# Token-major projections in chunks of 512 columns instead of 256, one PSUM bank for each block of 128 tokens

## The chip, the core and the metric

The kernel runs on one core of one Trainium2 chip. The metric is the device time of one execution in microseconds (us). In what follows PE is TensorE, DVE is VectorE, ACT is ScalarE, POOL is GpSimd and SP is SyncE, whose queue issues the DMAs.

## The reference, cut to what matters

Four layers work on 512 tokens of 1024 features in float32: an even mixer, a retention mixer and two hybrid mixers, each followed by a gated convolutional feed-forward network. Every layer begins with a normalisation of the features and ends with a residual. What matters here are the projections at the head of each mixer and the attention that reads them:

```python
# even mixer
proj = xn @ w_in
q, k, v, gate_b, gate_c, h = jnp.split(proj, ...)
q = rms_norm(heads(q), q_gain); k = rms_norm(heads(k), k_gain)
a = dilated_attention(q, k, heads(v))
b = gate_b * causal_dwconv(gate_c * h, sconv_w)
return jnp.concatenate([a, b], axis=-1) @ w_out
# retention mixer
o = chunkwise_retention(rotary(xn @ wq), rotary(xn @ wk), xn @ wv)
return (jax.nn.silu(xn @ wg) * group_norm(o)) @ wo
# hybrid mixer (two layers)
q_nsa, kv_nsa, g_nsa, qkv_sb, g_merge = jnp.split(h @ w_in, cuts, axis=-1)
o_nsa = nsa_attention(rope(q_nsa), ...)        # compressed + selected + window, gated
o_sb = stick_breaking_attention(*qkv_sb)
g_a, g_b = jnp.split(jax.nn.sigmoid(g_merge), 2, axis=-1)
y = g_a * (o_nsa @ w_proj_nsa) + g_b * (o_sb @ w_proj_sb)
return y @ w_out
```

## The kernel before, in words

The kernel is written in stages: mix0, ffn0, mix1, ffn1, hyb0, glu0, hyb1, glu1. The activations stand transposed in SBUF, as eight tiles of 128 features by 512 tokens; xgh and xgl are their high and low parts. Every matrix product is made of three matmuls (`mm3`): high by high, high by low, low by high. Weights arrive by DMA as units of 1024 columns (`unit`: raw, three buffers), ACT casts them to whi and DVE subtracts to get wlo (four buffers each).

There are two kinds of projection. `lin_a` is feature-major: the weights are the stationary operand and 512 tokens move, one PSUM bank for a result of 128 features by 512 tokens. `lin_b` is token-major: 128 tokens of the activations are the stationary operand and the weights' columns move. A chunk of `lin_b` has 256 columns and all four blocks of 128 tokens; two blocks share a bank, so a chunk takes two banks, and 96 matmuls (eight k-tiles, four blocks, three products). In a unit the loop goes over token blocks outside and k-tiles inside; while the first weights are still arriving (`ahead`) it goes over k-tiles outside. Token-major chunks: six in mix0 (q, q, k, k, v, v), four for each of the four heads of mix1 (two for v by `tok_split`, two for the gate), six in each hybrid layer (two of keys and values w[2] and w[3], then w_in_c with 280 columns, which already takes four banks, two of q, and two of the stick-breaking v by `tok_pack`).

PSUM has eight banks under four names with two buffers each: pa, psc, ptr and po. Within a name the banks go round in the order of the code. In the attention stages psc takes the scores, ptr the transposes, po the products with v, and pa the projections. In the hybrid layers the code has first the keys, values, q, then the compressed, selected and window attention (scores on psc; `softmax`, `pv`), then `tok_pack` of the stick-breaking v, then five gate projections (`gate`, `lin_a` on pa), and then the stick-breaking attention (`heads` with `sticks`), whose own q and k projections are also `lin_a` on pa.

The order on each engine is set by a scheduler that lets an instruction go as soon as its inputs, buffers and banks are free, so a projection that stands later in the code runs earlier, between the matmuls of the attention, where its banks allow it. On the chip each engine runs its row in that order.

At the start, SP brings x and the first weights in turn (`run`), with 256 columns for each of eight k-tiles; DVE casts these first weights instead of ACT. After the first chunk `norm` makes the factor rc of each token (sixteen small matmuls on ptr), by which each evacuation multiplies.

Of the kernel before, what the change touches and what calls it, by code (L numbers as in the profile page):

```python
# [69 lines left out]
class Kern:  # L70
# [147 lines left out]
    def lin_b_halves(self, ws, xs, banks):  # L218
        res = []
        parts = []  # L220
        for w, bank in zip(ws, banks):
            parts.append([self.unit(w[:, k:k + 4, :], UNIT) for k in range(0, KT, 4)])
            b = [x() for x in bank]
            res.append(([b[tb // 2][:, tb % 2 * 256:tb % 2 * 256 + 256] for tb in range(4)], b))
        for h in range(2):
            for k in range(KT):
                sl = slice(k % 4 * 256, k % 4 * 256 + 256)
                for j, (outs, _) in enumerate(res):
                    wh, wl = parts[j][k // 4]
                    for tb in (2 * h, 2 * h + 1):  # L230
                        tsl = slice(tb * 128, tb * 128 + 128)
                        self.mm3(outs[tb], tuple(z[:, tsl] for z in xs[k]), (wh[:, sl], wl[:, sl]),
                                 k == 0 and tb % 2 == 0, k == KT - 1 and tb % 2 == 1)
                if k % 2 == 1:
                    self.chain_step()
            self.chain_end()
        return res


    def lin_b(self, w, xs, bank=None):  # L240
        cols = w.shape[2]
        per = UNIT // cols
        if cols <= 256:
            bank = bank or self.pa
            banks = [bank(), bank()]
            outs = [banks[tb // 2][:, tb % 2 * 256:tb % 2 * 256 + cols] for tb in range(4)]
        else:
            banks = [self.pa(), self.pa(), self.po(), self.po()]
            outs = [b[:, :cols] for b in banks]
        for k in range(0, KT, per):  # L250
# [4 lines left out]
            for tb, q in order if early else sorted(order):  # L255
                xh, xl = xs[k + q]
                sl = slice(q * cols, q * cols + cols)
                tsl = slice(tb * 128, tb * 128 + 128)
                self.mm3(outs[tb], (xh[:, tsl], xl[:, tsl]), (wh[:, sl], wl[:, sl]),
                         k + q == 0 and (cols > 256 or tb % 2 == 0), k + q == KT - 1 and (cols > 256 or tb % 2 == 1))  # L260
        return outs, banks
# [201 lines left out]
    def tcols(self, toks, c0, n, tb):  # L463
        return toks[c0 // 256][tb // 2][:, tb % 2 * 256 + c0 % 256:tb % 2 * 256 + c0 % 256 + n]
# [147 lines left out]
    def tok_evac(self, banks, name="tok"):  # L612
        out = []
        for b in range(2):
            t = self.slot(name=name)
            self.nc.vector.tensor_tensor(t.rearrange("p (b c) -> p b c", b=2), banks[b].rearrange("p (b c) -> p b c", b=2),
                                         self.rc[:, 2 * b:2 * b + 2, None].to_broadcast([128, 2, 256]), ALU.mult)
            out.append(t)
        return out


    def tok_split(self, w, name="v", bank=None):
        out = [(self.slot(512, F32R, name + "h"), self.slot(512, F32R, name + "l")) for _ in range(4)]
        for c in range(2):
            sl = slice(c * 256, c * 256 + 256)
            ps, _ = self.lin_b(w[c], self.xs, bank and bank[c])
            for tb in range(4):
                self.split_to(out[tb][0][:, sl], out[tb][1][:, sl], ps[tb], self.rc[:, tb:tb + 1])
        return out
# [19 lines left out]
    def mix0(self, nxt):  # L649
        nc, a = self.nc, self.a  # L650
        w, xs = a["even_w_in_b"], self.xs
        rp, rt, rf, rc = self.ring(10), self.ring(6), self.ring(4), self.ring(2)
# [4 lines left out]
        toks = [[], []]  # L657
        for c in range(4):
            _, banks = self.lin_b(w[c], xs, (self.pa, self.psc)[c % 2])
# [4 lines left out]
            for b in range(2):  # L664
                t, sq = self.slot(name="qk"), rf.get(name="sq")
                nc.scalar.copy(t, banks[b])
# [3 lines left out]
                b3 = lambda t: t.rearrange("p (b h) -> p b h", b=2)  # L670
                rs = slice(2 * b, 2 * b + 2)
                nc.vector.tensor_tensor(b3(ss), b3(ss), r2[:, rs, None].to_broadcast([128, 2, 4]), ALU.mult)
                rr = self.rstd(ss, 8, 1.0 / 64, "rh")
                nc.vector.tensor_tensor(b3(rr), b3(rr), self.rc[:, rs, None].to_broadcast([128, 2, 4]), ALU.mult)
# [3 lines left out]
            toks[c // 2].append(row)  # L678
        v = self.tok_pack([w[4], w[5]])

        def prep(p):
            r = (self.stack_q(rq.get, self.transp(toks[0], p * 128), gg[:, 0:1], "q"),
                 self.stack_k(rq.get, self.transp(toks[1], p * 128), "k"))
            if p % 2 == 1:
                self.free([t[p // 2] for t in toks])
# [27 lines left out]
    def mix1(self, nxt):  # L713
# [65 lines left out]
        for h in range(4):  # L779
            v = self.tok_split([a["ret_wv"][2 * h + c] for c in range(2)], bank=(self.pa, self.psc))  # L780
            at, box = weigh(h, rot)
            gs = [self.slot(name="g") for _ in range(4)]
            for c in range(2):
                ps, _ = self.lin_b(a["ret_wg"][2 * h + c], xs, (self.pa, self.psc)[c])
                for tb in range(4):
                    nc.scalar.activation(gs[tb][:, c * 256:c * 256 + 256], ps[tb], AF.Silu, scale=self.rc[:, tb:tb + 1])
# [71 lines left out]
    def rope(self, dst, src, b, nh, rf):  # L858
# [4 lines left out]
        t4 = f4(t.rearrange("p (b c) -> p b c", b=2)[:, :, :nh * 64])  # L863
        cos = self.cos[:, 2 * b:2 * b + 2, None, :].to_broadcast([128, 2, nh, 32])
        sin = self.sin[:, 2 * b:2 * b + 2, None, :].to_broadcast([128, 2, nh, 32])
# [53 lines left out]
    def hyb(self, l, post, nxt):  # L919
# [13 lines left out]
        cmpt = self.tok_evac(banks, "cm")  # L933
        for b in range(2):
            kr = rf.get(name="kr")
            nc.vector.tensor_copy(b2(kr)[:, :, 0:128], b2(cmpt[b])[:, :, 0:128])
            self.rope(b2(cmpt[b])[:, :, 0:128], b2(kr)[:, :, 0:128], b, 2, rf)
        gbk = self.blocks([cmpt], 0, "ck", l, rf)
        gbv = self.blocks([cmpt], 128, "cv", l, rf)
# [3 lines left out]
        def kv_branch(ps, banks, name):  # L943
# [6 lines left out]
            for b in range(2):  # L950
                self.rope(b2(ktok[b])[:, :, 128:256], b2(ktok[b])[:, :, 0:128], b, 2, rf)
            k = self.stack_k(self.slot, self.transp([ktok], 128), name)
# [3 lines left out]
        kvs = [kv_branch(*(slc if self.halved else self.lin_b(w[3], xs, self.psc)), "ks")]  # L956
        ps, banks = self.lin_b(a["w_in_c"][l], xs)
# [3 lines left out]
        kvs.append(kv_branch(ps, banks, "kw"))  # L961
# [3 lines left out]
        qs = []  # L965
        for c in range(2):
            _, banks = self.lin_b(w[c], xs, (self.psc, self.pa)[c])
            raw = self.tok_evac(banks, "qraw")
# [200 lines left out]
def lay_b(w):  # L1169
    return w.reshape(KT, 128, w.shape[1]).transpose(1, 0, 2)  # L1170
# [115 lines left out]
```

## Time and profile before

| | us |
|---|---|
| median of three runs | 3037.67 |
| lowest and highest | 3032.94, 3037.71 |
| the profiled execution | 3034.34 |
| span of its instructions | 3032.6 |
| PE busy | 2959.9 (98%) |
| DVE busy | 1918.4 (63%) |
| ACT busy | 1389.0 (46%) |
| POOL busy | 293.4 (10%) |

Times in the trace are counted from the start of the span. A matmul's time is from its start to a modelled end, and matmuls overlap, so what one costs in a dense stretch is the distance of two starts.

### The profile page before, as it was taken

To read this page: it belongs to the slowest core of one execution; us is meant where nothing else is said; L and a number is where in the kernel's file an instruction comes from. 1 tells how busy PE (TensorE), PEld (TensorE's weight loads), DVE (VectorE), ACT (ScalarE), POOL (GpSimd) and SP (SyncE) were. 2 spreads that over 40 slices of the span, in tenths; PEclk is the share of its full clock that TensorE was granted. 3 is DMA by queue.
4 is the path that set the end of the run, shared out by engine and by line. 5 is a ranking of instruction groups with operands and counts; after the bars stand their busy time and mean duration, and the time that the engine had idled before them with its cause. 6 is when DMAs were issued, how large, how long until landed. Compare 5 with 4: busy or idle time off the path is not lost.

```text
span 3032.6 us, 39902 instructions
## 1 busy us (share of the span) xinstructions
PE 2959.9 (98%) x15620; PEld 2523.6 (83%) x15620; DVE 1918.4 (63%) x3077; ACT 1389.0 (46%) x2293; POOL 293.4 (10%) x306
## 2 busy tenths in 40 slices
PE   8999999999999999999998999999999989999998
PEld 8888888899889788889886788888888768888887
DVE  6877774344554677635889548774278794587733
ACT  4744443333333444324687335443356773454432
POOL 1010000111110100011003012000130030110001
PEclk9999999999999999999999999999999999999999
DMA  4122233322222222333111332223231112233232
GB/s 146 62 84 94 95 97 95 110 88 81 84 80 78 90 97 96 98 113 124 51 42 36 111 105 84 97 98 93 90 129 43 45 53 96 99 98 97 96 95 67
DMA packets 84380, 268.09 MB, mean 88 GB/s; under 512 B 9824, under 2 KB 13536, under 8 KB 84192
## 3 DMA queue, kind: packets, MB, share of 16 engines
q1 hardware_dynamic: 84192, 265.55, 27.1%
q8 instruction: 123, 2.02, 0.3%
q14 instruction: 65, 0.53, 0.1%
HBM read 258.17 MB, written 6.29 MB: 87 GB/s over the span
## 4 chain that ended last, share of the span: by engine, by line
PE 84%; DVE 7%; issue 4%; ACT 2%; POOL 2%; DMA 0%; SPq 0%; POOLq 0%; DVEq 0%; ACTq 0%
PE pa L159 38%; PE psc L159 24%; PE po L159 12%; PE ptr L159 8%; PE ptr L558 1%; DVE m L428 1%; DVE x L433 1%; POOL acc L304 1%; DVE wlo L155 1%; DVE cu L541 1%; DVE xgl L278 1%; ACT p L519 0%; POOL om L537 0%; DVE rb L334 0%; PE ptr L470 0%
## 5 line engine op out<-in xcount | busy, mean ns | idle before, releaser
L155 DVE TENSOR_TENSOR wlo<-raw,whi 128x1024 fp32r<-128x1024 f32 (+3 forms) x500 | 593.0, 1188 | 468.9 <-ACT whi L154 464.8
L154 ACT CAST whi<-raw 128x1024 fp32r<-128x1024 f32 (+2 forms) x492 | 494.8, 1006 | 807.9 <-PE pa L159 267.4
L159 PE MATMUL pa<-xgh,whi 128*128 128x512 f32 (+1 forms) x1344 | 521.6, 388 | 0.1
L159 PE MATMUL pa<-xgl,whi 128*128 128x512 f32 (+1 forms) x1344 | 520.4, 387 | 0.0
L159 PE MATMUL pa<-xgh,wlo 128*128 128x512 f32 (+1 forms) x1344 | 520.1, 387 | 0.0
L159 PEld LDWEIGHTS pa<-xgh,whi 128*128 128x128 f32 x1344 | 253.4, 189 | 47.0 <-DVE rt L733 0.5
L159 PEld LDWEIGHTS pa<-xgh,wlo 128*128 128x128 f32 x1344 | 253.3, 188 | 47.0
L159 PEld LDWEIGHTS pa<-xgl,whi 128*128 128x128 f32 x1344 | 253.3, 188 | 46.3
L304 POOL TENSOR_TENSOR acc<-acc,sq 128x512 f32<-128x512 f32 x78 | 126.5, 1622 | 1695.9 <-ACT sq L302 1694.3
L159 PE MATMUL psc<-xgl,whi 128*128 128x512 f32 x672 | 262.1, 390 | 1.0 <-DVE xgl L278 1.0
L159 PE MATMUL psc<-xgh,whi 128*128 128x512 f32 x672 | 262.2, 390 | 0.3 <-ACT xgh L277 0.3
L159 PE MATMUL psc<-xgh,wlo 128*128 128x512 f32 x672 | 261.6, 390 | 0.0
L159 PE MATMUL pa<-whi,xgh 128*128 128x256 f32 (+1 forms) x672 | 194.6, 290 | 6.4 <-ACT acc L295 5.4
L159 PE MATMUL pa<-wlo,xgh 128*128 128x256 f32 (+1 forms) x672 | 194.3, 289 | 4.8 <-DVE wlo L155 4.6
L159 PE MATMUL pa<-whi,xgl 128*128 128x256 f32 (+1 forms) x672 | 193.3, 288 | 0.0
L274 ACT CAST hh<-y 128x512 fp32r<-128x512 f32 x88 | 54.5, 620 | 221.9 <-DVE y L389 221.9
L159 PEld LDWEIGHTS psc<-xgl,whi 128*128 128x128 f32 x672 | 126.3, 188 | 27.2 <-DVE xgl L278 1.3
L159 PEld LDWEIGHTS psc<-xgh,whi 128*128 128x128 f32 x672 | 126.3, 188 | 26.6 <-ACT xgh L277 0.7
L159 PEld LDWEIGHTS psc<-xgh,wlo 128*128 128x128 f32 x672 | 126.2, 188 | 25.9
L159 PEld LDWEIGHTS pa<-whi,xgh 128*128 128x128 f32 x672 | 131.1, 195 | 7.6 <-ACT acc L295 5.3
L159 PE MATMUL ptr<-hl,whi 128*128 128x512 f32 x352 | 137.1, 389 | 0.0
L159 PE MATMUL ptr<-hh,whi 128*128 128x512 f32 x352 | 137.1, 389 | 0.0
(396 smaller groups left out, 6238.3 us busy)
## 6 DMA issues: line engine op xcount, KB each, us to landing
raw<-ffn_w_up SPq DMA_DIRECT2D x88, 512.0 KB, 3.5
raw<-w_up SPq DMA_DIRECT2D x88, 512.0 KB, 3.5
raw<-w_in_a SPq DMA_DIRECT2D x48, 512.0 KB, 3.2
raw<-ffn_w_down SPq DMA_DIRECT2D x32, 512.0 KB, 3.5
raw<-w_down SPq DMA_DIRECT2D x32, 512.0 KB, 3.5
raw<-w_in_b SPq DMA_DIRECT2D x24, 512.0 KB, 3.7
raw<-ret_wv SPq DMA_DIRECT2D x16, 512.0 KB, 3.6
raw<-ret_wg SPq DMA_DIRECT2D x16, 512.0 KB, 3.5
```

The lines of the kernel that those rows point to most:

```text
L154: (nc.vector.tensor_copy if step < n else nc.scalar.copy)(hi[:, cs], raw[:, cs])
L155: nc.vector.tensor_tensor(lo[:, cs], raw[:, cs], hi[:, cs].bitcast(F32), ALU.subtract)
L159: self.nc.tensor.matmul(out, l, r, start=start, stop=stop)
L274: nc.scalar.copy(hi, src)
L278: nc.vector.scalar_tensor_tensor(lo, src, scale, hi.bitcast(F32), ALU.mult, ALU.subtract)
L304: nc.gpsimd.tensor_tensor(st["sum"][0][:, hs], st["sum"][0][:, hs], sq[:, hs], ALU.add)
L428: nc.vector.tensor_tensor(m, m, rb[:, :256], ALU.mult)
L433: nc.vector.tensor_tensor(x, x, m, ALU.add)
L541: nc.vector.tensor_tensor_scan(cu[:, :n][:, ::-1], r, r, 1.0, ALU.mult, ALU.min)
L558: nc.tensor.transpose(t[:, c:c + 128], ps[e][i][:, j * 128:j * 128 + 128], self.ident)
```

## The change

`lin_b` and `lin_b_halves` take chunks of 512 columns and one bank for each block of 128 tokens, so four banks for a chunk, which the caller names. Two chunks of 256 columns become one of 512, with 96 matmuls as one had before. Evacuations read a bank of one token block with 512 columns; rope takes one token block with eight heads for q; the layouts of the weights on the host follow. A unit of 1024 columns now holds two k-tiles. Three raw buffers instead of two are filled ahead at the start, with six of the eight k-tiles. In the hybrid layers w[1] holds the 512 columns of both key and value chunks, and the stick-breaking v is one chunk on two pa and two psc banks, where it had been two chunks on pa.

```diff
-    def lin_b(self, w, xs, bank=None):
+    def lin_b(self, w, xs, banks):
         cols = w.shape[2]
         per = UNIT // cols
-        if cols <= 256:
-            bank = bank or self.pa
-            banks = [bank(), bank()]
-            outs = [banks[tb // 2][:, tb % 2 * 256:tb % 2 * 256 + cols] for tb in range(4)]
-        else:
-            banks = [self.pa(), self.pa(), self.po(), self.po()]
-            outs = [b[:, :cols] for b in banks]
+        outs = [bank()[:, :cols] for bank in banks]
...
-    def tok_pack(self, w, out=None):
+    def tok_pack(self, w, bank, out=None):
         out = out or self.v_tiles()
-        for c in range(2):
-            ps, _ = self.lin_b(w[c], self.xs)
-            for tb in range(4):
-                self.pack(out[tb][c], ps[tb], self.rc[:, tb:tb + 1])
+        for tb, p in enumerate(self.lin_b(w, self.xs, bank)):
+            for c in range(2):
+                self.pack(out[tb][c], p[:, c * 256:c * 256 + 256], self.rc[:, tb:tb + 1])
...
     def mix0
-        for c in range(4):
-            _, banks = self.lin_b(w[c], xs, (self.pa, self.psc)[c % 2])
+        for c, bank in enumerate(([self.pa, self.pa, self.psc, self.psc], [self.po, self.po, self.ptr, self.ptr])):
+            ps = self.lin_b(w[c], xs, bank)
...
-        v = self.tok_pack([w[4], w[5]])
+        v = self.tok_pack(w[2], [self.pa, self.pa, self.po, self.po])
...
     def mix1
-            v = self.tok_split([a["ret_wv"][2 * h + c] for c in range(2)], bank=(self.pa, self.psc))
+            v = self.tok_split(a["ret_wv"][h], [self.po, self.po, self.pa, self.pa])
...
-            for c in range(2):
-                ps, _ = self.lin_b(a["ret_wg"][2 * h + c], xs, (self.pa, self.psc)[c])
-                for tb in range(4):
-                    nc.scalar.activation(gs[tb][:, c * 256:c * 256 + 256], ps[tb], AF.Silu, scale=self.rc[:, tb:tb + 1])
+            ps = self.lin_b(a["ret_wg"][h], xs, [self.ptr, self.ptr, self.pa, self.pa])
+            for tb in range(4):
+                nc.scalar.activation(gs[tb], ps[tb], AF.Silu, scale=self.rc[:, tb:tb + 1])
...
     def hyb
-        if self.halved:
-            (_, banks), slc = self.lin_b_halves([w[2], w[3]], xs, [(self.psc, self.pa), (self.psc, self.pa)])
-        else:
-            _, banks = self.lin_b(w[2], xs)
+        lin = self.lin_b_halves if self.halved else self.lin_b
+        pkv = lin(w[1], xs, [self.psc, self.psc, self.pa, self.pa])
...
-        ps, banks = self.lin_b(a["w_in_c"][l], xs)
+        ps = self.lin_b(a["w_in_c"][l], xs, [self.po, self.po, self.pa, self.pa])
...
-        for c in range(2):
-            _, banks = self.lin_b(w[c], xs, (self.psc, self.pa)[c])
-            raw = self.tok_evac(banks, "qraw")
+        for tb, p in enumerate(self.lin_b(w[0], xs, [self.psc, self.psc, self.po, self.po])):
+            raw = rf.get(name="qraw")
+            nc.vector.tensor_scalar(raw, p, self.rc[:, tb:tb + 1], None, ALU.mult)
...
-        self.tok_pack([w[4], w[5]], v)
+        self.tok_pack(w[2], [self.pa, self.pa, self.psc, self.psc], v)
...
     def run
-                c = k % 4 * 256
-                nc.sync.dma_start(raws[k // 4][:, c:c + 256], a["even_w_in_b"][0][:, k, :])
-                if k % 4 == 3:
-                    self.ahead.append((raws[k // 4], 256))
+                c = k % 2 * 512
+                nc.sync.dma_start(raws[k // 2][:, c:c + 512], a["even_w_in_b"][0][:, k, :])
+                if k % 2 == 1:
+                    self.ahead.append((raws[k // 2], 512))
```

The scheduler makes a new order of it. PE in the attention stage of hyb0, from the transposes of the compressed attention on, before (pc and sT are tiles of the compressed attention, ks and kw keys, pa_13496 is a bank of the stick-breaking v):

```order
L1031 MATMUL ptr_12269<-ident,pc_12257 128x128 x4
L1013 MATMUL ptr_12289<-ident,sT_12287 128x128 x4
L159 MATMUL psc_12365<-ks_11652,q_12017 128x384
L159 MATMUL psc_12365<-ks_11654,q_12017 128x384
L159 MATMUL psc_12370<-ks_11652,q_12017 128x512
L159 MATMUL psc_12370<-ks_11654,q_12017 128x512
L159 MATMUL po_12444<-pcTh_12274,vc_12205 128x512
L159 MATMUL pa_13496<-whi_13500,xgl_10932 128x256
L159 MATMUL pa_13496<-whi_13500,xgh_10652 128x256
L159 MATMUL pa_13496<-wlo_13501,xgh_10652 128x256
```

PE at the same place after the change (p are the weights of the softmax, vp and vc values):

```order
L1003 MATMUL ptr_11003<-ident,pc_10991 128x128 x4
L159 MATMUL psc_11096<-kw_10614,q_10843 128x384
L159 MATMUL psc_11096<-kw_10616,q_10843 128x384
L159 MATMUL psc_11101<-kw_10614,q_10843 128x512
L159 MATMUL psc_11101<-kw_10616,q_10843 128x512
L550 MATMUL ptr_11147<-ident,p_11016 128x128
L159 MATMUL po_11142<-pcTh_11008,vc_10902 128x512
L550 MATMUL ptr_11147<-ident,p_11019 128x128
L550 MATMUL ptr_11147<-ident,p_11016 128x128
L550 MATMUL ptr_11147<-ident,p_11015 128x128
L159 MATMUL po_11142<-pcTl_11009,vc_10902 128x512
```

The matmuls of v on pa are gone from between the scores; 48 of its 96 stand ahead of the first scores of the stage, the other 48, on psc, at its end, and the gate projections come after them.

ACT at the start, from the last square of x on, before (qk<-pa is an evacuation of the first chunk, whi a cast of weights of the second):

```order
L302 ACTIVATE sq_166<-x_91 128x512
L666 COPY qk_309<-pa_174 128x512
L154 CAST whi_339<-raw_337 128x1024
L283 ACTIVATE sd_297<-ptr_292,eps 128x4
L667 ACTIVATE sq_310<-qk_309 128x512
```

ACT at the same place after the change:

```order
L292 ACTIVATE sq_165<-x_91 128x512
L154 CAST whi_269<-raw_267 128x1024
L154 CAST whi_372<-raw_370 128x1024
L154 CAST whi_402<-raw_400 128x1024
L154 CAST whi_432<-raw_430 128x1024
L644 COPY qk_314<-pa_173 128x512
```

One cast of the first chunk and three of the second now stand ahead of the first evacuation.

## Rows read from the trace of the kernel before

**Rows 1.** The page: busy us, share, instructions; granted clock; chain's shares by engine.
```profile
PE 2959.9 (98%) x15620; PEld 2523.6 (83%) x15620; DVE 1918.4 (63%) x3077; ACT 1389.0 (46%) x2293; POOL 293.4 (10%) x306
...
PEclk9999999999999999999999999999999999999999
...
PE 84%; DVE 7%; issue 4%; ACT 2%; POOL 2%; DMA 0%; SPq 0%; POOLq 0%; DVEq 0%; ACTq 0%
```

**Rows 2.** Timeline, PE, mix1 and ffn0: start, duration, engine, line, operation, tiles, shape.
```profile
622.28 0.28 PE L159 MATMUL pa<-whi,xgh 128*128 128x256 f32 x1
...
633.79 0.28 PE L159 MATMUL psc<-whi,xgh 128*128 128x256 f32 x1
...
300.00 0.39 PE L159 MATMUL pa<-xgl,whi 128*128 128x512 f32 x1
...
309.97 0.39 PE L159 MATMUL psc<-xgh,whi 128*128 128x512 f32 x1
```

**Rows 3.** Groups by form, PE: count, busy us, mean ns, idle before, releaser.
```profile
L159 PE MATMUL pa<-whi,xgh 128*128 128x256 f32 x640 | 185.2, 290 | 5.9 <-ACT acc L295 5.4 <-ACT xgh L277 0.6
...
L159 PE MATMUL psc<-whi,xgh 128*128 128x256 f32 x448 | 127.9, 286 | 1.6 <-ACT xgh L277 1.4
...
L159 PE MATMUL pa<-whi,xgh 128*128 128x280 f32 x32 | 9.5, 296 | 0.4 <-DVE vp L278 0.4
```

**Rows 4.** Timeline of mix0's six chunks, PE, then ACT; idle time and releaser in brackets.
```profile
5.37 0.77 PE L159 MATMUL pa<-whi,xgh 128*128 128x256 f32 x2 [5.37 <-ACT acc L295]
...
18.31 0.38 PE L159 MATMUL pa<-wlo,xgh 128*128 128x256 f32 x1 [2.70 <-DVE wlo L155]
...
26.97 0.95 PE L159 MATMUL ptr<-one,acc 128*128 128x1 f32 x8
...
29.51 1.72 PE L159 MATMUL ptr<-ident,rc 128*128 128x128 f32 x8
...
89.43 0.82 PE L470 MATMUL ptr<-ident,qk 128*128 128x128 f32 x6
...
26.45 0.59 ACT L666 COPY qk<-pa 128x512 f32<-128x512 f32 x1 [10.31 <-PE pa L159]
26.93 1.05 ACT L154 CAST whi<-raw 128x1024 fp32r<-128x1024 f32 x1
```

**Rows 5.** Windows, attention stages of hyb0, hyb1: length, PE, PEld, DVE, ACT, POOL, clock, DMA.
```profile
1465.90:1573.40 107.50, 106.06 (x639) 90.18 (x640) 93.90 (x292) 85.33 (x206) 2.58 (x2) 1.00 0.11 40
2289.00:2396.50 107.50, 106.05 (x638) 90.17 (x639) 93.74 (x292) 85.22 (x206) 2.58 (x2) 1.00 0.11 40
```

**Rows 6.** Groups by form within 1465.9 to 1573.4 us, PE.
```profile
L159 PE MATMUL pa<-xgh,whi 128*128 128x512 f32 x41 | 16.7, 406 | 0.0
...
L159 PE MATMUL pa<-whi,xgl 128*128 128x256 f32 x39 | 11.0, 282 | 0.0
```

**Rows 7.** The same groups within 1465.9 to 1573.4 us, DVE.
```profile
L155 DVE TENSOR_TENSOR wlo<-raw,whi 128x1024 fp32r<-128x1024 f32 x7 | 8.5, 1219 | 0.0
...
L278 DVE SCALAR_TENSOR_TENSOR vp<-pa,rc,vp 128x256 fp32r<-128x256 f32 x8 | 3.8, 480 | 1.0 <-ACT vp L277 1.0
L1073 DVE TENSOR_TENSOR ga<-pa,rb 128x512 f32<-128x512 f32 x4 | 2.7, 672 | 0.0
```

**Rows 8.** Windows: densest stretch of the attention stage, and the sticks stage, hyb0.
```profile
1470.00:1512.40 42.40, 41.30 (x283) 36.97 (x282) 40.47 (x128) 31.16 (x83) 2.58 (x2) 1.00 0.10 33
1590.00:1686.00 96.00, 86.68 (x418) 65.83 (x417) 87.46 (x138) 66.24 (x140) 29.79 (x64) 0.98 0.18 55
```

**Rows 9.** Windows around two long waits of PE, in mix1 and in hyb0.
```profile
705.50:709.00 3.50, 1.65 (x15) 1.45 (x14) 2.72 (x4) 1.18 (x2) 0.16 (x1) 1.00 0.44 145
709.00:712.40 3.40, 3.40 (x18) 3.40 (x18) 1.43 (x2) 0.89 (x3) 0.00 (x0) 0.50 0.02 5
1408.70:1412.10 3.40, 1.64 (x14) 1.44 (x13) 3.40 (x11) 2.29 (x6) 1.16 (x2) 1.00 0.06 23
```

More of the change, by code (lines that the diff above doesn't have):

```diff
@@ L215, in chain_end, with lin_b_halves @@
             self.chain_step()
[L218 to L224, printed above, removed]
+    def lin_b_halves(self, w, xs, banks):
+        cols = w.shape[2]
+        per = UNIT // cols
+        parts = [self.unit(w[:, k:k + per, :], UNIT) for k in range(0, KT, per)]
+        outs = [bank()[:, :cols] for bank in banks]
         for h in range(2):
             for k in range(KT):
[L227 to L233, printed above, removed]
+                wh, wl = parts[k // per]
+                sl = slice(k % per * cols, k % per * cols + cols)
+                for tb in (2 * h, 2 * h + 1):
+                    tsl = slice(tb * 128, tb * 128 + 128)
+                    self.mm3(outs[tb], tuple(z[:, tsl] for z in xs[k]), (wh[:, sl], wl[:, sl]), k == 0, k == KT - 1)
                 if k % 2 == 1:
@@ L663, in mix0 @@
             row = []
-            for b in range(2):
+            for tb, p in enumerate(ps):
                 t, sq = self.slot(name="qk"), rf.get(name="sq")
-                nc.scalar.copy(t, banks[b])
+                nc.scalar.copy(t, p)
                 nc.scalar.activation(sq, t, AF.Square)
@@ L683, in prep @@
                  self.stack_k(rq.get, self.transp(toks[1], p * 128), "k"))
-            if p % 2 == 1:
-                self.free([t[p // 2] for t in toks])
+            if p == 3:
+                self.free(toks)
             return r
@@ L932, in hyb @@
         causal = self.table("causal")
-        cmpt = self.tok_evac(banks, "cm")
+        cmpt = [self.slot(name="cm") for _ in range(2)]
+        for tb in range(4):
+            nc.vector.tensor_scalar(b2(cmpt[tb // 2])[:, tb % 2, :], pkv[tb][:, 0:256], self.rc[:, tb:tb + 1], None, ALU.mult)
         for b in range(2):
@@ L1123, in run @@
                  "hyb0": "g_pre_mix0", "glu0": "g_pre_ffn0", "hyb1": "g_pre_mix1", "glu1": "g_pre_ffn1"}
[L1125 removed]
+        raws = [self.wpool.tile([128, UNIT], F32, tag="raw", name=self.nm("raw"), bufs=3) for _ in range(3)]
         for k in range(KT):
             nc.sync.dma_start(self.x[k], a["xT"][k])
[L1128 to L1132 removed]
+            if stages[0] == "mix0" and k < 6:
+                c = k % 2 * 512
+                nc.sync.dma_start(raws[k // 2][:, c:c + 512], a["even_w_in_b"][0][:, k, :])
+                if k % 2 == 1:
+                    self.ahead.append((raws[k // 2], 512))
         nc.sync.dma_start(self.ident, a["ident"])
@@ L1211, in layout @@
     w = g["even_w_in"][0]
-    o["even_w_in_b"] = np.stack([lay_b(w[:, i * 256:i * 256 + 256]) for i in range(6)])
+    o["even_w_in_b"] = np.stack([lay_b(w[:, i * 512:i * 512 + 512]) for i in range(3)])
     o["even_w_in_a"] = lay_a(w[:, 1536:])
@@ L1217, in layout @@
     for n in ("ret_wv", "ret_wg"):
-        o[n] = np.stack([lay_b(g[n][0][:, h * 256:h * 256 + 256]) for h in range(8)])
+        o[n] = np.stack([lay_b(g[n][0][:, h * 512:h * 512 + 512]) for h in range(4)])
     t = lay_a(g["ret_wo"][0])
@@ L1230, in layout @@
         b = np.concatenate([q[:, perm], kv[:, :512], sb[:, 1024:]], 1)
-        wb.append(np.stack([lay_b(b[:, i * 256:i * 256 + 256]) for i in range(6)]))
+        wb.append(np.stack([lay_b(b[:, i * 512:i * 512 + 512]) for i in range(3)]))
         wc.append(lay_b(np.concatenate([kv[:, 512:], gt], 1)))
```

82 lines of the change are left out of this document (33 added, 49 removed).

## The prediction

> **What bounds the kernel now.** I read the page first. TensorE (PE) is busy for 98% of the span and the chain of work that ended last runs through it for 84%, at the full clock nearly everywhere [rows 1]. So any term must be read as PE time: what the change takes from PE's queue, and where it leaves PE idle. Second, the timeline, to see what one matmul costs there. The durations overlap, so the cost is the spacing of starts. In a token-major stretch of mix1, 96 matmuls of 256 columns start between 622.28 and 633.79 us: 0.1199 us each. In the feed-forward stage, 44 matmuls of 512 columns start between 300.00 and 309.97 us: 0.2266 us each [rows 2]. Third, the groups by form for the counts [rows 3]. Fourth, the windows of two places where PE is not simply a queue: the start of the kernel [rows 4] and the attention stage of the hybrid layers [rows 5 to 8].
>
> **Part 1, fewer matmuls.** The 256-column token-major groups hold three forms of 640 and three of 448 [rows 3], 3264 matmuls, which become 1632 of 512 columns. Two of 0.1199 less one of 0.2266 leave 0.0132 us, so 1632 x 0.0132 = **21.5 us less** on PE, all of it on the path as long as PE is dense. The weights are cut into the same units of 1024 columns, so casts, their subtractions on VectorE (DVE) and bytes stay. The w_in_c chunk (280 columns) stays as it was. The evacuations become half as many and twice as wide; their fixed costs fall on DVE and ScalarE (ACT), which do not bound the dense stages: nothing.
>
> The Trainium skill, "TensorE: Matmul & The Clock Gate", section "Back-to-back issue gap", gives for an isolated matmul the columns at 2.4 GHz plus 2.5 ns. By that a pair would save 2.5 ns and this term would be 4.1 us. The spacings here are wider than it says at both sizes, and their difference is what counts; it comes back below as a rival.
>
> **Part 2, the start.** From the first matmul at 5.37 us to the first transpose at 89.43 us [rows 4] lie 84.1 us. The 576 matmuls of the six chunks are 69.1 us at 0.1199, the 16 small matmuls of the norm 2.7 us (0.95 and 1.72), so 12.3 us go to waits and half clock. The rows show two causes: the first chunk waits for DVE's wlo (2.70 us at one place), and the second chunk waits for a weight cast that stands on ACT behind an evacuation (26.45, then 26.93 us). After the change each k-tile has 12 matmuls of 512 columns, 2.7 us of PE at full clock for three DVE operations, where it had 1.4 us for three; and the order puts the casts of the second chunk ahead of the first evacuation. PE should wait little for DVE, but it still starts at half clock. The gain lies between 0 and 12.3 us. I take **8 us**, nearer the upper end, because both causes are touched and the cold start stays.
>
> **Part 3, the attention stage of the hybrid layers.** This term decides. From 1465.90 to 1573.40 us (compressed, selected and window attention of layer 0) PE is covered throughout, DVE is busy 93.90 us of 107.5 and ACT 85.33; layer 1 is the same to 0.2 us [rows 5]. But much of PE's work there is not attention: 122 matmuls of gate projections (three forms, 41, 41 and 40) and 115 token-major ones of the next v (39, 38 and 38) [rows 6], 122 x 0.2266 + 115 x 0.1199 = 41.4 us. They write pa banks alone and fill every gap that the softmax leaves. What remains of PE is 107.5 - 41.4 = 66.1 us, its short waits included.
>
> Now the v chunk takes two banks of pa and two of psc. The scores of the attention rotate through the same two psc banks, and the v chunk stands behind them in the code, so its psc half can't begin before the last score is read; its pa half can, and then holds both pa banks and all four weight buffers until the psc half is done. The gates behind it wait for both. The order shows it: the filler between the scores is gone; 48 pa matmuls stand ahead of the stage, the gates behind it. So 41.4 us of PE work leave a stage that can shrink only to what DVE needs.
>
> DVE without the filler's own part (weight subtractions 8.5, v 3.8, gates 2.7 us [rows 7]) is 93.9 - 15.0 = 78.9 us. At 100% that is the stage's floor. At the density it had over the whole stage (93.90/107.5 = 87%) the stage takes 90.4 us; at the best stretch of it (40.47/42.40 = 95% [rows 8]) 82.7 us. I take 91%, halfway, since PE will answer sooner but each DVE step still hangs on a score from PE and an exponential from ACT: 87 us. The stage's loss is its new length less the PE work that stays: 87 - 66 = 21 us, with 17 to 24 from the two densities, 13 at the floor, and 41 if it should keep its length. For two layers **+42 us**. The moved work hides nothing on the way: in the dense stretch behind the stage PE is alone, and the next stage (sticks) has its own fillers.
>
> **Part 4, seams and clock.** Each chunk now takes four banks, so a chunk that follows may wait for an evacuation. The nearest row is the 280-column chunk, already on four banks: 0.4 us in all for a bank [rows 3]. With some twenty seams the bounds are 0 and 8 us; I take **+2**, near the row. The clock falls to half after long idle times: from 709.00 to 712.40 us it is 0.50, behind a stretch in which PE was covered for 1.65 of 3.50 us; 1.64 of 3.40 us from 1408.70 us on left it at 1.00 [rows 9]. A stage with PE idle for a quarter of its time (66 of 87 us used) will see a few of these. The fall in the row is 3.4 us long and costs at most half of that, 1.7 us, less what DVE hides; I take **+3** for both layers, between 0 and 7.
>
> **Sum.** Against the profiled execution (span 3032.6 and 1.7 us around it, 3034.3 us, which is 3.3 below the median of 3037.67 and inside the range of its three runs): 3034.3 - 21.5 - 8 + 42 + 2 + 3 = 3051.8, **3052 us**.
>
> **Rivals.**
> (a) Not slower: DVE closes up. The gains are 21.5 + 8 us; the stage cancels them where it takes 66.1 + 14.8 = 80.9 us with no cost in part 4, that is, from a DVE density of 97.5% on. For it: without filler ahead of them the scores come sooner, and DVE has less to wait for. Against: even the best stretch was at 95%. At 79 us and no cost in part 4 it gives 3034.3 - 29.5 + 25.8 = 3031 us; at 95% with the whole 12.3 us of the start 3034. Chance 0.15.
> (b) The moved work finds other gaps. The sticks stage has 96.0 us with PE covered 86.68 [rows 8]; if the gates filled these 9.3 us in each layer, the result would be 3052 - 19 = 3033 us. Against: the order has the gates ahead of the first sticks, because later projections share their banks in turn. Chance 0.07.
> (c) The clock oscillates. If PE ran the stage at half clock for half of the time, its 66 us would be 99 and bind, (99 - 87) x 2 = 24 us more, 3076 us; at half clock throughout 132, and 3142 us. Against: the stretch from 1408.70 us, with PE idle for half of it, left the clock alone. The Trainium skill, same page, section "A second HAM failure mode: psum-queue depth-cycling", tells of a kernel whose short idle times between groups of matmuls did this; no stretch of this trace has such a pattern for long. Chance 0.09.
> (d) The change doesn't save what it says: 512 token-major columns cost nearly two of 256, a spacing of 0.237 us, the saving is 4 instead of 21.5 us, and 3069 us come out. Against: both spacings stand in rows 2. It is what the Trainium skill's section "Back-to-back issue gap" would give. Chance 0.04.
>
> **How the numbers follow.** The forecast has 0.65 and its own range is about 3040 to 3074: start 3 to 12.3, stage 17 to 24 a layer, seams and clock 0 to 15. To reach 8 in 10 the range goes from 3034 (the best density with the whole start) to 3078. Faster by over 0.2% of the median (under 3031.6) needs the floor of (a) or (b) with luck at the start: 0.08. Within 0.2%, about what a measurement of this kernel can tell from no change: the rest of (a) and (b) and the lower edge of the forecast, 0.17. Slower, over 3043.7: 0.75.
>
> **What will show it.** Part 1: spacing of 0.227 us in the token-major chunks, 1632 of them. Part 2: the first transpose 84.1 - 8 - 288 x 0.0132 = 72.3 us after the first matmul, near 78 us instead of 89.43. Part 3: a stage with no pa matmuls between the scores, 83 to 90 us long, DVE at 90% or more, PE in many waits of less than 1 us, and behind it five gate projections in one block. If that stage is over 95 us, or its clock row shows many halves, I sized it too low; if it is under 81 us, or PE has other work in it, the forecast of slower is wrong.

## The result, and the profile after

| | us |
|---|---|
| before, median of four runs beside it | 3036.22 (3032.94 to 3037.71) |
| after, median of four runs | 3070.51 (3069.18 to 3075.29) |
| ratio | 1.0117, 95% interval 1.0105 to 1.0130 |
| the profiled execution of after, and its span | 3071.68, 3070.0 |

The change costs 34 us. The forecast of 3052 us had the direction and the place, but only half of the size. From the page of the kernel after come PE's busy time, the granted clock in slices, and the chain's shares by engine; [rows 1] has the same lines of before.

```profile
PE 2966.4 (97%) x13988; PEld 2438.4 (79%) x13988; DVE 1918.6 (62%) x3060; ACT 1363.0 (44%) x2244; POOL 294.2 (10%) x306
...
PEclk9999999999999999999999999999998999999999
...
PE 80%; DVE 10%; issue 4%; ACT 4%; POOL 2%; DMA 0%; SPq 0%; POOLq 0%; DVEq 0%; ACTq 0%
```

PE has 1632 matmuls less, but the chain that ends last spends 4 points less on PE and 3 more on DVE: some place is now DVE's. The windows of the kernel after show which. The first is the attention stage of hyb0, then its head and its rest, the block behind it, and the stage of hyb1. Columns: length, then PE, PEld, DVE, ACT and POOL busy, clock, DMA share, GB/s.

```profile
1449.60:1545.00 95.40, 80.55 (x401) 60.13 (x401) 81.28 (x274) 63.70 (x181) 2.53 (x2) 0.91 0.00 1
1449.60:1476.00 26.40, 19.30 (x66) 14.98 (x66) 18.97 (x57) 11.68 (x32) 2.53 (x2) 0.69 0.00 1
1476.00:1545.00 69.00, 61.25 (x337) 45.15 (x335) 62.30 (x217) 52.02 (x151) 0.00 (x0) 1.00 0.00 1
1561.40:1607.80 46.40, 46.23 (x205) 37.99 (x205) 22.64 (x29) 20.30 (x28) 0.00 (x0) 1.00 0.32 103
2301.20:2395.30 94.10, 80.09 (x402) 59.34 (x402) 81.24 (x274) 63.69 (x181) 2.54 (x2) 0.91 0.00 1
```

A stage is counted here from the first score of the compressed attention to the last score of the window attention. Before, that was 105.7 us in hyb0 ([rows 5] run 1.9 us further) and held 39.85 us of filler, that is, projection matmuls counted at their spacings:

```profile
1465.80:1571.50 105.70, 104.25 (x630) 88.71 (x631) 92.04 (x287) 84.48 (x205) 2.58 (x2) 1.00 0.12 40
```

After, it is 95.4 and 94.1 us and holds none. Its DMA share is 0.00: no weights arrive in it. Behind it stands a block of 46.4 us in which PE does projections alone; that was 7.7 us.

The prediction has the gates waiting for pa and for the weight buffers. The timelines of the kernel after, of DVE and then of ACT, show pa free and the buffers held:

```profile
1450.02 1.01 DVE L268 SCALAR_TENSOR_TENSOR vp<-pa,rc,vp 128x256 fp32r<-128x256 f32 x2
...
1430.56 1.05 ACT L154 CAST whi<-raw 128x1024 fp32r<-128x1024 f32 x1 [4.39 <-PE po L159]
...
1550.80 1.05 ACT L154 CAST whi<-raw 128x1024 fp32r<-128x1024 f32 x1 [1.00 <-PE psc L159]
```

The last of v's pa banks is read out at 1451.0 us, 1.4 us into the stage, and no matmul writes pa again before 1566.2 us. But ACT casts no weights between 1430.56 and 1550.80 us: v's four units keep all four weight buffers until the psc half, behind the last score, has used the first of them.

Cut at such events, the two executions differ by 37.2 us (the spans by 37.4). "Own" is the length less the projections at their spacings; the differences are taken before rounding:

| stretch | before | after | difference |
|---|---|---|---|
| mix0, to ffn0's norm | 242.8 | 234.9 | -8.0 |
| ffn0 to ffn1's norm, with mix1 | 784.2 | 774.2 | -10.0 |
| hyb0 and hyb1: projections at their spacings | | | -7.6 |
| hyb0, hyb1: ahead of the stage, own | 15.6, 23.9 | 18.2, 26.1 | +4.9 |
| hyb0, hyb1: attention stage, own | 65.9, 66.0 | 95.4, 94.1 | **+57.6** |
| hyb0, hyb1: all behind it, own | | | +0.3 |

### The profile page after: what moved, and what is told of

Its sections match the earlier page's. It is cut to its first block, busy times and chain, and to the rows that moved or that the text cites. A ratio compares the mean times of both kernels' runs of the same rounds, so it can differ in the third digit from the quotient of the medians.

```text
span 3070.0 us, 36584 instructions
## 1 busy us (share of the span) xinstructions
PE 2966.4 (97%) x13988; PEld 2438.4 (79%) x13988; DVE 1918.6 (62%) x3060; ACT 1363.0 (44%) x2244; POOL 294.2 (10%) x306
## 4 chain that ended last, share of the span: by engine, by line
PE 80%; DVE 10%; issue 4%; ACT 4%; POOL 2%; DMA 0%; SPq 0%; POOLq 0%; DVEq 0%; ACTq 0%
PE pa L159 35%; PE psc L159 20%; PE po L159 14%; PE ptr L159 10%; DVE p L516 1%; DVE p L509 1%; DVE m L418 1%; ACT p L511 1%; DVE cu L533 1%; DVE ptl L265 1%; POOL acc L294 1%; PE ptr L550 1%; DVE x L423 1%; DVE wlo L155 1%; DVE xgl L268 1%
## 5 line engine op out<-in xcount | busy, mean ns | idle before, releaser
L159 PE MATMUL ptr<-hh,wlo 128*128 128x512 f32 x352 | 137.0, 389 | 0.0
L353 DVE SCALAR_TENSOR_TENSOR y<-u,cols,y 128x510 f32<-128x510 f32 x176 | 131.7, 749 | 5.7
L352 DVE SCALAR_TENSOR_TENSOR y<-u,cols,y 128x511 f32<-128x511 f32 x176 | 131.0, 745 | 4.6 <-ACT y L349 4.1
L159 PE MATMUL po<-hl,whi 128*128 128x512 f32 (+1 forms) x352 | 132.3, 376 | 0.0
```

The costliest lines, as they stand in the source:

```text
L159: self.nc.tensor.matmul(out, l, r, start=start, stop=stop)
L352: nc.vector.scalar_tensor_tensor(y[:, 1:T], u[:, 0:T - 1], self.col(w, i * 3 + 1), y[:, 1:T], ALU.mult, ALU.add)
L353: nc.vector.scalar_tensor_tensor(y[:, 2:T], u[:, 0:T - 2], self.col(w, i * 3), y[:, 2:T], ALU.mult, ALU.add)
```

## The experiments

All times are medians beside runs of the kernel before on the same chip (3034 to 3036 us).

**v alone in the kernel before.** The stick-breaking v becomes one chunk:

```diff
-        self.tok_pack([w[4], w[5]], v)
+        self.tok_pack_512(w[4], w[5], v)
...
+        ps = [self.pa(), self.pa(), self.psc(), self.psc()]
```

> The kernel before, with one part of the change alone: in the two hybrid layers the stick-breaking v is one chunk of 512 columns on two pa and two psc banks instead of two chunks of 256 on pa. Theory A (the two psc banks shut the filler out of the attention stage, and nothing else in the hybrid layers matters much): the traces before and after show 65.9 us for the stage's own work becoming 95.4 and 94.1 us, so +57.7 us for both layers, less 192 pairs x 0.0132 = 2.5 us: 3036 + 55 = 3091 us, 3080 to 3100. Rival B (the loss is shared with the single q chunk and the four-bank keys and values, which start the stage with a longer chain): about half, 3060 to 3070 us.

Measured 3081.6 us, ratio 1.0150 (1.0135 to 1.0165): +46, less than A's 55 and more than B's 25 to 35. The windows of both stages:

```profile
1464.50:1557.50 93.00, 80.96 (x417) 59.95 (x416) 81.04 (x275) 65.11 (x183) 2.57 (x2) 0.94 0.00 1
2313.00:2405.50 92.50, 80.10 (x417) 58.96 (x416) 80.91 (x274) 64.94 (x183) 2.58 (x2) 0.96 0.00 1
```

This one edit empties the stage: 3.4 us of filler are left, and the stage's own time grows by 23.7 and 23.1 us. The rest of the loss of the kernel after is not v's.

**v alone undone in the kernel after.**

```diff
-        self.tok_pack(w[2], [self.pa, self.pa, self.psc, self.psc], v)
+        self.tok_pack_256(w[2], v)
...
+        for c in range(2):
+            banks = [self.pa(), self.pa()]
```

> The kernel after, with this one part undone: the stick-breaking v of the hybrid layers is again two chunks of 256 columns on pa banks alone. Theory A: the stage has its 40 us of filler back; 3070.5 - 57.7 + 2.5 = 3015 us, 3008 to 3025, under both kernels. Rival B (the single q chunk and the wider keys and values have their own price in the hybrid layers): 3035 to 3050 us, since half of the loss stays.

Measured 3022.5 us, ratio 0.9958 (0.9943 to 0.9973), under both kernels, 7 us over A's number. The stage of hyb0 is covered again:

```profile
1449.40:1559.20 109.80, 108.58 (x631) 91.77 (x632) 91.86 (x288) 85.39 (x203) 2.59 (x2) 0.98 0.11 35
```

It holds 42.5 us of filler; its own time is 67.3 us. But ahead of it 18.5 and 27.7 us stay, where before had 15.6 and 23.9. That points at q.

**q alone undone in the kernel after.** v stays on pa and psc:

```diff
-        for tb, p in enumerate(self.lin_b(w[0], xs, [self.psc, self.psc, self.po, self.po])):
+        for c in range(2):
+            banks = self.lin_b_256(w[0], c, xs, (self.psc, self.pa)[c])
...
```

> The kernel after, with q of the hybrid layers back in two chunks of 256 columns (two psc banks, then two pa banks); the stick-breaking v stays one chunk on pa and psc. Theory C (the single q chunk has its own price: all of q's rope and stacking on DVE starts only behind its last matmul, and with no filler the attention stage starts on an empty PE): the kernel before with v alone changed lost 48.3 us in the hybrid layers where the kernel after lost 62.6 us, so 14.3 us come back, less 2.5 us for 192 pairs: 3059 us, 3055 to 3063. Rival A (only the psc banks of v count): 3070.5 + 2.5 = 3073, 3069 to 3075.

Measured 3058.9 us, ratio 1.0078 (1.0063 to 1.0093), as theory C has it. The window of hyb0's stage:

```profile
1442.80:1535.80 93.00, 80.40 (x417) 59.31 (x416) 81.07 (x275) 64.95 (x183) 2.57 (x2) 0.96 0.00 1
```

It is the 93 us of the first run, 3.4 us of filler among them. The single q chunk costs 11.6 us net of the 2.5 us that it saves: the stage's own time is 89.6 and 89.4 us here where it was 95.4 and 94.1, 10.5 us less, and 3.1 us less stand ahead of the stage of hyb0.

**Both undone in the kernel after.**

```diff
+            banks = self.lin_b_256(w[0], c, xs, (self.psc, self.pa)[c])
...
+        self.tok_pack_256(w[2], v)
```

> The kernel after, with both v and q of the hybrid layers back in two chunks of 256 columns (v on pa, q on psc and then pa); keys and values stay 512 wide. If the single q chunk also has a price where the stage has its filler (theory C: 18.5 and 27.7 us ahead of the stage in the run with v alone undone, 15.1 and 26.1 in the run with q alone undone, so 5 us for both layers, and up to 3 in the stage), 3022.5 - 5 + 2.5 = 3020 us, 3016 to 3021. If what counts is how much filler the order leaves in the stage (the run with v by pairs and q in 256 lost 7 us with 29.0 us of filler instead of 43.1, and 21.5 us of dense block behind the stage instead of 6.5), the time goes with the order: it has to have 40 us of filler again, and else it is slower, 3024 to 3030.

Measured 3017.6 us, ratio 0.9940 (0.9925 to 0.9955), in theory C's range. The stage is the one of before, 39.85 us of filler in 105.8 us, so the run doesn't tell C from the reading that the filler alone counts. Ahead of the stage of hyb1 nearly 3 us more stand than before the change; with v and q undone they belong to neither, and they were not followed up.

```profile
1444.90:1550.70 105.80, 104.34 (x631) 88.74 (x632) 92.05 (x287) 84.54 (x205) 2.59 (x2) 1.00 0.13 40
```

**The clock.** In the head of the stage after, the granted clock is 0.69. Matmuls with zeros were added to v's pa half (`fill` is 64 there), so that PE has something to run in the head:

```diff
+            for i in range(fill if k == KT - per else 0):
+                self.mm(outs[i % 2], self.zero, xs[0][0], False, False)
...
```

> The kernel after with 64 added matmuls of 512 columns with a stationary tile of zeros in the pa half of the stick-breaking v of each hybrid layer: they add nothing to the sums, and they are there to keep TensorE running where it waits at the head of the attention stage (granted clock 0.69 over 1449.6 to 1476.0 us). If the low clock of the head is what made the stage longer than the 87 us forecast, the head runs at 1.00 and each layer gains 2 to 6.5 us: 3057 to 3066 us. If the head is a chain of DVE, ACT and POOL steps whatever the clock, the time stays, 3068 to 3073. If the added work stands in the way of the scores, up to 128 x 0.2266 = 29 us more, 3099.

Measured 3068.9 us, ratio 1.0111 (1.0094 to 1.0128). The windows of the head and of the whole stage of hyb0:

```profile
1447.60:1473.20 25.60, 24.89 (x126) 19.65 (x127) 21.08 (x68) 14.55 (x39) 2.59 (x2) 1.00 0.01 1
1447.60:1541.00 93.40, 85.87 (x458) 64.73 (x459) 81.37 (x274) 64.55 (x181) 2.59 (x2) 1.00 0.00 1
```

The clock is at 1.00 throughout, and the stage still takes 93.4 us (hyb1 93.5), 2.0 and 0.6 us less. That need not be all of the clock's price, since 42 of the zeros and 12 matmuls of v, 12.2 us of PE, now run in the stage. A better mark is the second time that ACT reads the transposed weights of the compressed attention, first in the kernel after, then here:

```profile
1472.72 0.59 ACT L264 CAST pcTh<-ptr 128x512 fp32r<-128x512 f32 x1 [0.47 <-PE ptr L1003]
...
1467.72 0.59 ACT L268 CAST pcTh<-ptr 128x512 fp32r<-128x512 f32 x1 [0.72 <-PE ptr L1007]
```

That is 23.1 us into the stage and 20.1 us into it: up to there the zeros gave back 3.0 us (hyb1 1.7). The stage missed the forecast 87 us by 8.4, so the clock is at most a part of it. How much of the 3 us the added matmuls took back later was not separated.

**DVE's part.** The multiplication of the softmax weights is left out in the hybrid layers:

```diff
         for i, p in enumerate(ps):
-            nc.vector.tensor_scalar(p, p, rd[:, i:i + 1], None, ALU.mult)
+            if gate is None:
+                nc.vector.tensor_scalar(p, p, rd[:, i:i + 1], None, ALU.mult)
```

> The kernel after without the multiplication of the softmax weights by their factor on DVE in the hybrid layers (62 operations, 22.8 us of DVE time in each layer; the weights stay unnormalised and ungated). If DVE sets the length of the attention stage after the change, the stage shrinks until ACT (63.7 us busy in 95.4) or the chain binds: 11 to 22 us a layer, 3026 to 3048 us. If PE's half clock and the waits between the engines set it, 0 to 5 us a layer: 3060 to 3070.

Measured 3047.4 us, ratio 1.0038 (1.0023 to 1.0053): 23 us less than after. The windows of both stages:

```profile
1447.40:1530.30 82.90, 75.16 (x397) 59.51 (x397) 64.27 (x213) 61.45 (x175) 2.54 (x2) 0.90 0.00 1
2288.80:2370.20 81.40, 74.77 (x396) 58.68 (x396) 64.24 (x213) 61.37 (x174) 2.54 (x2) 0.90 0.00 1
```

DVE has 17 us less to do inside these bounds, and the stage shrinks by 12.5 and 12.7 us; DVE's density falls from 85% to 78%. The time came out in the range for DVE as what sets the stage. DVE carries most of the stage's length, but not as a queue that is always full: of 82.90 us it is busy 64.27 and ACT 61.45. PE is covered for 75.16, where a matmul's time reaches to its modelled end.

**Less than all the filler back.** Three gates ahead of v in the code, v still on pa and psc:

```diff
-        self.tok_pack(w[2], [self.pa, self.pa, self.psc, self.psc], v)
...
-        tas.extend(self.slot(name="ga") for _ in range(2))
         for n, g in enumerate(tas):
             gate(g, 8 + n)
+        self.tok_pack(w[2], [self.pa, self.pa, self.psc, self.psc], v)
+        for n in range(3, 5):
+            tas.append(self.slot(name="ga"))
+            gate(tas[n], 8 + n)
```

> The kernel after with three of the five gate projections ahead of the stick-breaking v in the code; v stays one chunk of 512 columns on pa and psc. The order of the kernel puts 24 gate and 48 v matmuls of 512 columns, 16.3 us, between the scores, where there are none. Theory A (each us of filler that goes back is a us less, as long as the stage doesn't get longer): 3070.5 - 2 x 16.3 = 3038 us, 3032 to 3045. Rival (the stage's own chain has its length and the filler makes it longer by as much as it is late): 3050 to 3065.

Measured 3048.4 us, ratio 1.0044 (1.0029 to 1.0059), just short of the rival's range and 10 us over theory A. The 16.3 us of filler lengthen the stages by 1.7 and 3.0 us, and 4 us more stand ahead of them. The window of hyb0's stage:

```profile
1448.10:1545.20 97.10, 89.65 (x476) 69.83 (x477) 84.12 (x278) 71.01 (x189) 2.59 (x2) 0.98 0.03 9
```

**512 columns without psc.** v by two blocks of 128 tokens at a time on two pa banks, alone and with q in 256 columns:

```diff
+        parts = [self.unit(w[:, k:k + 2, :], UNIT) for k in range(0, KT, 2)]
+        for h in range(2):
+            ps = [self.pa(), self.pa()]
...
```

> The kernel after, with the stick-breaking v in 512 columns still, but two blocks of 128 tokens at a time on the two pa banks, all four weight buffers kept through both halves. Theory A (only the banks matter, not the width): like the two chunks of 256 columns, 3022.5, less 2.5 us for the 192 pairs: 3020 us, 3015 to 3024. Rival (the four weight buffers are held until the second half is done, the gates behind get their weights late and the filler dries up): 3028 to 3045.

> The kernel after, with v by pairs of token blocks on pa and with q back in two chunks of 256 columns. With filler in the stage the single q chunk cost, by the run with v in 256 columns, 6.9 us ahead of the stage and 2.9 us in it over both layers; undone, less 2.5 us for its pairs, it gives 7.3 us: 3020 - 7 = 3013 us, 3008 to 3018 (theory C). Rival A (q doesn't matter): 3022.

Measured 3019.7 us (0.9947, 0.9931 to 0.9964) and 3027.1 us (0.9973, 0.9962 to 0.9984). The first is as forecast: the width is not the trouble. Nor are held buffers by themselves, since v keeps all four through both halves here too; but its second half, on pa, can run between the scores and then lets them go, where on psc it could not. The second run is a miss by 14 us. The windows show what changed: the stage of the first run in hyb0, then that of the second and the block behind it:

```profile
1447.30:1560.60 113.30, 110.91 (x590) 90.54 (x591) 93.71 (x287) 87.48 (x205) 2.59 (x2) 0.97 0.13 38
...
1442.10:1546.50 104.40, 98.21 (x540) 80.30 (x540) 91.28 (x289) 79.70 (x201) 2.57 (x2) 0.97 0.10 31
1559.70:1581.20 21.50, 21.36 (x96) 17.38 (x95) 12.13 (x16) 10.48 (x15) 0.00 (x0) 1.00 0.24 75
```

The new order left 29.0 us of filler in the stage, where v by pairs alone had 43.05, and a block of 21.5 us behind it. Why the scheduler did so was not tried.

**q by pairs too.** With v by pairs, q's first two token blocks are finished first:

```diff
-        for tb, p in enumerate(self.lin_b(w[0], xs, [self.psc, self.psc, self.po, self.po])):
+        for tb, p in enumerate(self.lin_b_halves(w[0], xs, [self.psc, self.psc, self.po, self.po])):
```

> The kernel after with v by pairs of token blocks on pa, and q in 512 columns but with its first two token blocks finished before the other two begin, so that half of its rope runs beside PE's second half. Theory C (q's rope and stacking behind its last matmul is the price of the single chunk): 3 to 5 us less than the 3019.7 of v by pairs alone, 3015 to 3018. Rival (the transposes need all four token blocks, and v's weights come later because q holds the four weight buffers): 3019 to 3025.

Measured 3016.3 us, ratio 0.9938 (0.9922 to 0.9955), in C's range; but its interval overlaps that of v by pairs alone, so the 3.4 us between the two times are not clear of noise. The traces are clearer: ahead of the stage 18.5 and 28.0 us were left with v by pairs alone, and 16.1 and 23.5 us are left here, as before the change, with every such chunk 512 wide.

**The start.** The sum of squares without POOL (`tail` says how many of the eight squares go to PE without an add):

```diff
-            st = self.ssq_add(st, k, self.x[k])
+            st = self.ssq_add(st, k, self.x[k], tail=KT - 1)
```

> The kernel after, with the sum of squares at the start left to PE (32 small matmuls of one column instead of 8) in place of the seven adds on POOL. In the trace after, DVE takes 1.51, 1.65 and 1.77 us between 9 and 20 us, while POOL adds, for casts, subtractions and scalings of 512 columns that take 0.43, 0.69 and 0.75 us before and after. If POOL's adds are what slows them, they take the short times throughout and PE's waits of 3.0 us in the first chunk go; 24 more small matmuls at 0.1 us are 2.4 us: 3070 us, 3067 to 3071. If it is the weights or the tokens that arrive then (DMA at its full rate from 6.4 to 15 us), DVE stays slow and the time is 3072 to 3075.

Measured 3079.4 us, ratio 1.0147 (1.0132 to 1.0162): half right, since DVE did get faster. On DVE's timeline of the kernel after (start, duration, operation) the operations on 512 columns are short ahead of POOL's adds, which run from 8.88 to 19.87 us, and long beside them:

```profile
5.88 0.43 DVE L154 CAST whi<-raw 128x512 fp32r<-128x512 f32 x1 [0.50 <-DMA raw<-even_w_in_b]
6.34 0.69 DVE L155 TENSOR_TENSOR wlo<-raw,whi 128x512 fp32r<-128x512 f32 x1
...
8.99 1.51 DVE L154 CAST whi<-raw 128x512 fp32r<-128x512 f32 x1
10.53 1.66 DVE L155 TENSOR_TENSOR wlo<-raw,whi 128x512 fp32r<-128x512 f32 x1
12.12 1.78 DVE L268 SCALAR_TENSOR_TENSOR xgl<-x,gains,xgh 128x512 fp32r<-128x512 f32 x1
```

On DVE's timeline of the experiment they stay short in the same stretch:

```profile
8.29 0.42 DVE L154 CAST whi<-raw 128x512 fp32r<-128x512 f32 x1
8.74 0.69 DVE L155 TENSOR_TENSOR wlo<-raw,whi 128x512 fp32r<-128x512 f32 x1
10.27 0.75 DVE L268 SCALAR_TENSOR_TENSOR xgl<-x,gains,xgh 128x512 fp32r<-128x512 f32 x1 [0.83 <-ACT xgh L267]
```

The first chunk took 23.4 us instead of 28.0. What the expectation had wrong is PE's part: 64 matmuls of one column and not 32, at 0.15 us and not 0.1, and the clock. They cost more than the first chunk gains: ffn0's norm comes at 240.9 us, 6.0 later than in the kernel after, and the rest of the loss arises in hyb1 and behind it, for no cause that a run shows. The windows of the experiment, of the last 56 of those small matmuls and of what follows:

```profile
30.60:38.90 8.30, 8.30 (x58) 8.30 (x56) 0.00 (x0) 0.66 (x2) 0.00 (x0) 0.73 0.00 1
38.90:41.90 3.00, 3.00 (x13) 2.71 (x13) 1.66 (x4) 1.71 (x3) 0.00 (x0) 0.50 0.01 3
```

**The best version.** v and q by pairs, and the adds at the start on DVE:

```diff
+            (add or nc.gpsimd).tensor_tensor(st["sum"][0][:, hs], st["sum"][0][:, hs], sq[:, hs], ALU.add)
...
+            st = self.ssq_add(st, k, self.x[k], add=nc.vector)
```

> The kernel after with three edits: v of the hybrid layers by pairs of token blocks on pa, q finished by pairs of token blocks (as in the run at 3016.3 us), and the seven adds of the sum of squares at the start on DVE instead of POOL. Without POOL's adds the first chunk took 23.4 us instead of 28.0 in the run that gave them to PE, whose own small matmuls then cost more than that. The seven adds take 0.69 us each on DVE, 4.8 us beside the 15 us of its other work there, and PE needs 2.7 us a k-tile: if DVE keeps ahead of PE, 3016.3 - 4 = 3012 us, 3010 to 3015, faster than both kernels. If the adds stand ahead of the weights that PE waits for, 3016 to 3020.

Measured 3012.5 us, ratio 0.9930 (0.9917 to 0.9944), faster than both kernels. The norm of ffn0 comes 1.7 us earlier than in the run at 3016.3, less than the 4 us expected of the start. The two intervals overlap, so the 3.8 us between the times are not clear of noise, and where the rest of them came from was not settled.

## Why the prediction was right, and where it was wrong

**Part 1 held.** In a token-major stretch of the kernel after, 15 matmuls start between 622.27 and 625.67 us, 0.2267 us each, against 0.2266 of [rows 2]:

```profile
622.27 0.39 PE L159 MATMUL pa<-whi,xgh 128*128 128x512 f32 x1
...
625.67 0.39 PE L159 MATMUL po<-whi,xgh 128*128 128x512 f32 x1
```

mix1 alone gives 768 x 0.0132 = 10.1 us by the term and 10.0 by the traces. Rival (d) falls.

**Part 2 was half right.** PE's timeline of the kernel after has the first matmul and the first transpose:

```profile
6.45 0.77 PE L159 MATMUL pa<-whi,xgh 128*128 128x512 f32 x1 [6.45 <-DVE whi L154]
...
80.11 0.39 PE L462 MATMUL ptr<-ident,qk 128*128 128x128 f32 x2
```

The transpose came at 80.11 and not near 78 us. From the first matmul to it are 73.7 us, where 72.3 were forecast, so by this sign 6.6 of the 8 us came; by ffn0's norm 4.2 are left beside part 1. The step that failed is that "PE should wait little for DVE". It rests on the count of DVE operations for a k-tile, and leaves out how long they take there: [rows 4] have PE waiting 2.70 us for a wlo, and DVE's timeline of the kernel before, of which the prediction uses no row, has a cast of 256 columns at 1.37 us in that stretch and at 0.28 behind it:

```profile
9.27 1.37 DVE L154 CAST whi<-raw 128x256 fp32r<-128x256 f32 x1
...
18.18 0.28 DVE L154 CAST whi<-raw 128x256 fp32r<-128x256 f32 x1
```

The run without POOL's adds shows what this costs: the first chunk takes 4.6 us less. The first matmul also came 1.1 us later, behind a cast that waits for weights of twice the size to arrive (5.88 us above), and 1.4 us more go between the first transpose and ffn0's norm, where no run shows why.

**Part 3 had the mechanism and three quarters of the size, and it is the step that made the number wrong.** Its term of +42 us measured +57.6. No filler between the scores, the gates in one block behind: that is what the trace shows, though the gates stood behind the weight buffers, with pa free. Two things were mis-sized, and the runs part the missing 15.6 us between them.

First, the empty stage, forecast at 87 us. With q in two chunks it took 93.0 and 92.5 us, 89.6 and 89.1 of them its own: a loss of 23.7 and 23.1 us where 21 was forecast, 5 us of the 15.6. The working divided DVE's own 78.9 us by 91%, between 87% and 95%, densities that were read from the stage with filler in it; but there 15.0 of DVE's 93.9 us were the filler's own evacuations and weights, which can use any gap. Without them its own work was 78.9/107.5 = 73% dense. Alone DVE was busy 81.0 to 81.3 us at 85 to 87%, and no denser at full clock or with less to do.

Second, the price of the q chunk, which part 1 set at nothing because evacuations fall on engines that "do not bound the dense stages". q's rope and stacking stand between its last matmul and the first score, and one chunk puts all of them there. Undoing it shortened the stages' own time by 10.5 us, the rest of the 15.6, and the whole by 3070.5 - 3058.9 = 11.6 us, 14 with its pairs. That it is the rope behind the last matmul, and not another effect of the order, is argued from the run that finishes q by pairs, not shown alone. With q undone the mark in the head comes 20.0 us into the stage, as it does with the zeros, so some of q's price may be the clock's.

How the stage's length goes with its filler, from the runs above (us, hyb0):

| filler | 0 | 3.4 | 16.3 | 29.0 | 39.85 | 42.5 | 43.05 |
|---|---|---|---|---|---|---|---|
| stage | 95.4 | 93.0 | 97.1 | 104.4 | 105.8 | 109.8 | 110.7 |

The runs differ in q too: one chunk at 0, 16.3 and 42.5 us, two at 3.4, 29.0 and 39.85, one finished by pairs at 43.05. So 0 and 16.3 can be compared, and there 16 us of filler are nearly free; at 40 us the stage is its own 66 us and the filler, and PE is full.

**Part 4** forecast 5 us for seams and clock, and 5.2 came ahead of the stage and behind it. That the sums agree is luck: 3.1 of the 5.2 us go when q is undone, and what the clock cost lies inside the stage. Rival (a) falls: DVE did not close up. Rival (b) falls: the sticks stage kept its length, 72.5 us before and 72.7 after from its first score to its last, and the moved work stood ahead of it. Rival (c), the clock, did come, 0.69 over the head of the stage, but the run with zeros gave back 3.0 and 1.7 us up to the mark in the head and not 12 a layer. Its sum has a slip: half clock for half of the time makes 88 us of 66, and 99 is half clock for half of the work. The low ends of the forecast's own range add up to 3034.5 and not 3040.

With the measured terms, which is bookkeeping and no test, the sum is 3034.3 - 21.5 - 4.2 + 57.6 + 5.2 = 3071.4 us against the 3071.7 of the profiled execution.

## What to carry to other kernels

A wider tile that needs banks of another name ties its work to that name's users, and the buffers that it holds meanwhile tie up whatever stands behind it: ask which stage fills its gaps with the tile, and whether all of it can still run there. Two banks used twice kept both the width and the filler here. A density that an engine reaches with independent work mixed in is no middle estimate of what it reaches on a dependent chain alone: the 87% of the mixed stage was the most that the chain alone came to here, and the chain's own 73% in it the least. And of a chunk that is merged, count what now stands behind its last matmul.

## What the runs showed of the hardware

POOL's timeline of the kernel after has the seven adds of the start in one row:

```profile
8.88 10.99 POOL L294 TENSOR_TENSOR acc<-acc,sq 128x512 f32<-128x512 f32 x7 [8.38 <-ACT sq L292]
```

They lengthened DVE's operations beside them by about 1.0 to 1.1 us each, whatever these were: casts 0.43 to 1.51, subtractions 0.69 to 1.66, scalings 0.75 to 1.78 us. In the run that gave the adds to PE the three stay at 0.42, 0.69 and 0.75 us, and in the best version, where DVE does the adds, at 0.42, 0.68 and 0.74.

The Trainium skill, "SBUF — State Buffer", section "Who interferes with whom", states that a DVE instruction with two SBUF inputs contends with a GpSimd instruction that reads SBUF, that DVE in a two-port mode (which copies and casts can enter) contends with GpSimd too, and that the one that issues first blocks the other for its whole instruction. The trace agrees that all three kinds get longer. They do so by less than one add (10.99/7 = 1.57 us); which of the two began first, and in which mode the casts ran, the rows don't tell.

In the run without POOL's adds, PE was busy by the profile in the 8.30 us of its one-column matmuls, and yet the granted clock was 0.73 there and 0.50 (1.2 GHz) in the 3.0 us behind them.
